# A diffusion trunk of two layers: the second layer's strips requested one to a step from the context's fifteenth step on, and four of its eight normalised beside later products

## Chip, cores and metric

The kernel runs on one core of a Trainium2 chip. Its time is in device microseconds (us), from one execution to the next of the same program; the number compared is the median of three runs. The profile is of one further execution, and all places in it are given in us from the start of its span.

## The reference

A trunk of two layers works on 1024 latent tokens of width 1024 (a grid of 16 rows of 64) with 256 context tokens before them. The first layer mixes tokens by attention and a linear recurrence, the second by neighbourhood attention on the grid. Around each mixer and each feed-forward part stand a root-mean-square norm and a modulation (scale and shift, computed from a conditioning vector). What the change touches is the end of the first layer's feed-forward part and the start of the second layer:

```python
# layer 0, end: feed-forward part of the latent and the context tokens
x   = x   + g2  * rms_norm(conv_ffn(h_lat, ...), norm_post_ffn[0])
ctx = ctx + g2c * rms_norm(conv_ffn(h_ctx, ...), norm_post_ffn[0])
# layer 1, start
h_lat = rms_norm(x,   norm_pre_mix[1]) * (1.0 + sc1)  + sh1
h_ctx = rms_norm(ctx, norm_pre_mix[1]) * (1.0 + sc1c) + sh1c
qkv   = h_lat @ w_qkv        # and h_ctx @ w_qkv; the values v are computed first
```

All matrix products are made from three products of halves (hi by hi, hi by lo, lo by hi): a tile read from memory, the raw tile, is split by ScalarE (ACT), which casts the high half, and by VectorE (DVE), which subtracts it for the low half.

## The kernel before

TensorE (PE), ACT, DVE, GpSimd (POOL) and the queue of SyncE (SP), which issues nearly all loads, each run their instructions in the order in which the program was written. In the part at hand that holds for SP too: a request that has to wait holds up every request behind it. Requests on SP take one of eight completion semaphores in turn, so that a request also waits until the one that last used its semaphore has landed.

**The down projection of the first layer** (`ffn_down`) ends with the context tokens, which are done as 22 steps, one for each block of 128 rows of the weight (`d_rawB`, 512 KB). I number them 0 to 21. A step has 12 matmuls: 2 blocks of tokens by 2 halves of the columns by 3. Its high and low halves are `d_Bh`, `d_Bl` (weight) and `d_Ah`, `d_Al` (activations, read from `actd` once for four steps, `d_rawA`, 512 KB). The products of the steps 18 to 21 are written as one pass of 48 matmuls at step 18; the 12 positions of the loop after that have no products. At each step the program also prepares the split four steps ahead and requests the weight two steps further ahead. `d_rawB` has three buffers, so the request for step k waits until the split of step k-3 has ended. The places for the halves of weights go round five.

Meanwhile the finished latent rows leave: DVE scales them and adds the old rows (`y`, `y_x`), and POOL issues their store into the scratch tensor `x2d`. When the context's products have ended, four pieces (`d_ps`, two blocks by two halves) are squared by ACT (line 1581), copied by DVE (line 1707), scaled and stored in turn. The accumulators come free with the last copy.

**The second layer's input** is `x2d`, read as eight strips `n_x` of 128 rows each, 512 KB (line 1733). Strip i holds every eighth row, beginning with row i, because the second layer works on 8 by 8 patches of the grid; so each strip needs all eight stores of latent rows. A strip is normalised in place by `odd_norm`: ACT squares and sums it (`junk`, line 1742), DVE adds epsilon (`rs_e`, line 120), POOL takes the power (`rs_r`, line 121), DVE multiplies (line 1745). `odd_norm` is a generator that gives way once for each strip and twice more.

`odd_early` is that work as a generator; the loop of the context's steps advances it once in each step (`next(other)`), after the step's other requests.

**`odd_values`** computes the second layer's values. `modulate(0, (0, 1, 2, 3), 0)` transposes the first four strips on PE (`n_pt<-ident,n_x`), ACT applies scale and shift (`n_t`), DVE splits (`xh`, `xl`). Eight weight pieces `w_raw` (512 KB, three buffers) are split into `w_hi`, `w_lo`. `products` multiplies tiles of 128 tokens: 24 matmuls a tile and half of the columns (`g_ps`), in eight yields of three matmuls. `mixed` takes one turn from each of its generators, and `both(a, b, n)` one turn of `b` after every n yields of `a`. The second four strips are modulated beside the products of the first four, the context tiles 8 and 9 beside those of the second four.

Of the kernel before, what the change touches and what calls it, by code (L numbers as in the profile page):

```python
# [13 lines left out]
BF16 = mybir.dt.bfloat16  # L14
# [6 lines left out]
P = 128  # L21
D = 1024
# [38 lines left out]
class Trunk:  # L61
# [1688 lines left out]
    def odd_early(self, nx, junk):  # L1750

        self.odd_x = {}
        for _ in range(9):
            yield
        for i in range(8):
            self.odd_load(nx, i)
        for _ in range(2):
            yield
        yield from self.odd_norm(range(8), junk)

    def odd_values(self, nx, xh, xl, gp, tp, sp):

        nc, a = self.nc, self.a
        sh, sc = self.mod[1, 0], self.mod[1, 1]
        wv = a["w_qkv"].rearrange("(k p) n -> p k n", p=P)
        raws, W = {}, {}

        def load(m):  # L1770
            if m < 8:
                raws[m] = self.wp.tile([P, 1024], F32, name="w_raw", bufs=3)
                k, c = 2 * (m % 4), 2048 + 512 * (m // 4)
                nc.sync.dma_start(raws[m].rearrange("p (a b) -> p a b", a=2), wv[:, k:k + 2, c:c + 512])

        def prepare(m):
            raw = raws.pop(m)
            hi, lo = (self.wp.tile([P, 1024], F32R, name="w_" + x, bufs=8) for x in ("hi", "lo"))
            nc.scalar.copy(hi, raw)
            nc.vector.tensor_tensor(out=lo, in0=raw, in1=hi.bitcast(F32), op=OP.subtract)  # L1780
            W[m] = hi, lo
            load(m + 3)

        def modulate(n0, tiles, s):
            n = P * len(tiles)
            for k in range(KT):
                pt = tp.tile([P, 512], F32, name="n_pt", tag="tp")
                for i, t in enumerate(tiles):
                    nc.tensor.transpose(pt[:, i * P:(i + 1) * P], self.odd_x[t][:, k * P:(k + 1) * P], self.ident)
                t = sp.tile([P, 512], F32, name="n_t", bufs=2)  # L1790
                nc.scalar.activation(t[:, :n], pt[:, :n], AF.Identity, scale=sc[:, k, s:s + 1], bias=sh[:, k, s:s + 1])
                nc.vector.tensor_copy(xh[:, k, n0:n0 + n], t[:, :n])  # L1792
                nc.vector.tensor_tensor(out=xl[:, k, n0:n0 + n], in0=t[:, :n], in1=xh[:, k, n0:n0 + n].bitcast(F32),
                                        op=OP.subtract)
                yield

        late = []

        def leave(ps, t, c):
            vs = sp.tile([P, 8, 2, HD], F32R, name="cv_st", bufs=2)  # L1800
            pv = ps.rearrange("p (h e) -> p h e", h=8)
            nc.scalar.copy(vs[:, :, 0, :], pv)
            yield
            nc.vector.tensor_tensor(out=vs[:, :, 1, :], in0=pv, in1=vs[:, :, 0, :].bitcast(F32), op=OP.subtract)
            yield
            nc.gpsimd.dma_start(self.vcd[t][:, 1024 * c:1024 * (c + 1)].bitcast(F32), vs.rearrange("p a b c -> p (a b c)").bitcast(F32))

        def products(tiles):

            for c in range(2):  # L1810
                for t in tiles:
                    ps = gp.tile([P, 512], F32, name="g_ps")
                    for k in range(KT):
                        wh, wl = (w[:, 512 * (k % 2):512 * (k % 2) + 512] for w in W[4 * c + k // 2])
                        xhk, xlk = xh[:, k, t * P:(t + 1) * P], xl[:, k, t * P:(t + 1) * P]
                        self.mm(ps, xhk, wh, k == 0, False)
                        self.mm(ps, xhk, wl, False, False)
                        self.mm(ps, xlk, wh, False, k == KT - 1)
                        if late and next(late[0], "end") == "end":
                            late.pop(0)  # L1820
                        yield
                    late.append(leave(ps, t, c))

        def both(a, b, n):

            for i, _ in enumerate(a):
                if i % n == n - 1:
                    next(b, None)
            for _ in b:
                pass  # L1830

        def mixed(*gens):
            gens = list(gens)
            while gens:
                for g in list(gens):
                    if next(g, "end") == "end":
                        gens.remove(g)
                    yield

        def context():  # L1840
            for i in (8, 9):
                self.odd_load(nx, i)
            junk = sp.tile([P, D], BF16, name="junk", bufs=1)
            yield
            yield
            yield from self.odd_norm((8, 9), junk)
            yield from modulate(SEQ, (8, 9), 1)

        def splits():
            for m in range(4, 8):  # L1850
                yield prepare(m)

        with self.in_order(*self.compute, mybir.EngineType.SP):
            for m in range(3):
                load(m)
            first = products((0, 1, 2, 3))
            for k, _ in enumerate(modulate(0, (0, 1, 2, 3), 0)):
                if k % 2 == 0:
                    prepare(k // 2)
                if k >= 2:  # L1860
                    next(first)
            both(first, mixed(splits(), modulate(512, (4, 5, 6, 7), 0)), 4)
            both(products((4, 5, 6, 7)), context(), 3)
            both(products((8, 9)), iter(()), 1)
            for g in late:
                for _ in g:
                    pass
# [445 lines left out]
```

## Time and profile before

| what | value |
|---|---|
| runs | 3455.88, 3460.55, 3461.36 us; median 3460.55 us |
| profiled execution | 3454.39 us |
| span of its trace | 3452.5 us, 48745 instructions |
| PE busy | 3137.3 us (91% of the span) |
| DVE, ACT, POOL busy | 2060.1, 1485.8, 1528.3 us |
| the part at hand | context's steps and the change of layer, about 1953 to 2140 us |

The profiled execution lies 6.2 us below the median of the runs, and its span 1.9 us below its own time. In the views, "idle before <-X" is the time in which an engine stood still before an instruction, with what ended it; `SPq` is SP's queue of requests; `PE` rows are matmuls and `PEld` rows the loads of the stationary operand beside them. The shares of the whole span say little on a part of 190 us; the part is read from the rows of that part.

### The profile page before, as it was taken

What the parts mean: (1) busy time and instruction counts of PE and PEld (TensorE: products, weight loads), DVE (VectorE), ACT (ScalarE), POOL (GpSimd) and SP (SyncE); (2) the same over time, 40 slices, a digit from 0 to 9 for tenths busy, and PEclk for the clock granted to TensorE, in tenths of its full rate; (3) what the DMA queues carried; (4) which work ended last, traced back from release to release, by engine and by line L of the source; (5) the groups of instructions that cost most, each with busy time, mean ns of one, the idle gap of its engine ahead of it and who ended that gap; (6) DMA issues with size and microseconds to landing.
All of it is one profiled execution on the core that took longest, in us unless ns stands there. A gap on an engine that the chain in (4) does not pass through costs nothing.

```text
span 3452.5 us, 48745 instructions
## 1 busy us (share of the span) xinstructions
PE 3137.3 (91%) x18364; PEld 2560.9 (74%) x18364; DVE 2060.1 (60%) x3413; ACT 1485.8 (43%) x2619; POOL 1528.3 (44%) x1147
## 2 busy tenths in 40 slices
PE   5999998869997799999999969999997689999997
PEld 3766776658886588888888748898986468888785
DVE  3625666657775745444577852477775565454778
ACT  3223222266663534343344442466674344333443
POOL 1310111187774476666510111577771167777201
PEclk7999999889999799999999989999999799999998
DMA  6533333321113112121285662222215412222756
GB/s 231 159 104 128 129 112 114 120 69 39 50 44 103 61 68 72 68 72 67 98 286 207 238 199 111 70 64 61 68 44 181 143 56 85 73 86 80 264 184 216
DMA packets 203948, 399.25 MB, mean 116 GB/s; under 512 B 23216, under 2 KB 85168, under 8 KB 203712
## 3 DMA queue, kind: packets, MB, share of 16 engines
q1 hardware_dynamic: 194656, 364.15, 32.0%
q0 software_dynamic: 9056, 31.99, 2.4%
q8 instruction: 144, 2.36, 0.3%
q14 instruction: 92, 0.75, 0.1%
HBM read 322.11 MB, written 74.34 MB: 115 GB/s over the span
## 4 chain that ended last, share of the span: by engine, by line
PE 73%; DVE 11%; DMA 5%; ACT 4%; issue 4%; POOL 2%; SPq 0%; POOLq 0%; ACTq 0%; DVEq 0%
PE g_ps L113 21%; PE u_g L113 13%; PE d_ps L113 10%; PE u_v L113 10%; PE u_pc L113 3%; PE a_pv L113 2%; PE c_pv L113 2%; PE c_s L113 2%; PE c_pt L2022 2%; PE a_pt L926 2%; PE mod_ps L113 1%; DVE a_pl L928 1%; PE a_s L113 1%; DMA d_rawA<-actd 1%; DMA y_x<-x2d 1%
## 5 line engine op out<-in xcount | busy, mean ns | idle before, releaser
L121 POOL TENSOR_TENSOR rs_r<-rs_e,mhalf 128x1 f32<-128x1 f32 (+3 forms) x106 | 84.8, 800 | 1019.8 <-DVE rs_e L120 1019.7
L113 PE MATMUL d_ps<-d_Bh,d_Ah 128*128 128x512 f32 x704 | 276.5, 393 | 28.1 <-ACT d_Ah L1456 21.9
L113 PE MATMUL g_ps<-xh,w_hi 128*128 128x512 f32 (+1 forms) x704 | 277.4, 394 | 6.4 <-ACT w_hi L543 6.4
L113 PE MATMUL d_ps<-d_Bl,d_Ah 128*128 128x512 f32 x704 | 277.4, 394 | 4.3 <-DVE d_Bl L1457 4.2
L113 PE MATMUL d_ps<-d_Bh,d_Al 128*128 128x512 f32 x704 | 276.4, 393 | 2.1 <-DVE d_Al L1457 1.9
L906 POOL TENSOR_SCALAR a_p<-a_p,rl 128x1280 f32<-128x1280 f32 (+1 forms) x80 | 240.1, 3004 | 70.5 <-DVE rl L905 62.3
L2005 POOL TENSOR_SCALAR c_p<-c_p,rl 128x640 f32<-128x640 f32 (+1 forms) x128 | 230.8, 1804 | 85.1 <-DVE rl L2004 60.5
L113 PE MATMUL g_ps<-xh,w_lo 128*128 128x512 f32 (+1 forms) x704 | 258.0, 367 | 1.2 <-DVE w_lo L544 1.2
L113 PE MATMUL g_ps<-xl,w_hi 128*128 128x512 f32 (+1 forms) x704 | 257.9, 366 | 0.0
L1238 DVE TENSOR_TENSOR f_u<-u_v,f_p 128x512 f32<-128x512 f32 x88 | 60.6, 688 | 199.0 <-PE u_v L113 199.0
L113 PEld LDWEIGHTS d_ps<-d_Bh,d_Ah 128*128 128x128 f32 x704 | 133.5, 190 | 57.8 <-ACT d_Ah L1456 23.2
L928 DVE TENSOR_TENSOR a_pl<-a_pt,a_ph 128x512 fp32r<-128x512 f32 (+1 forms) x200 | 118.6, 602 | 88.3 <-ACT a_ph L927 87.9
L113 PEld LDWEIGHTS g_ps<-xh,w_hi 128*128 128x128 f32 x704 | 134.3, 191 | 45.8 <-issue 27.5
L1224 POOL TENSOR_TENSOR w_S4l<-w_s,w_S4h 128x512 fp32r<-128x512 f32 x44 | 57.2, 1301 | 242.0 <-ACT w_S4h L1223 242.0
L113 PEld LDWEIGHTS d_ps<-d_Bl,d_Ah 128*128 128x128 f32 x704 | 133.3, 189 | 36.7 <-DVE d_Bl L1457 8.7
L113 PE MATMUL g_ps<-w_hi,xh 128*128 128x512 f32 (+1 forms) x400 | 156.6, 391 | 2.2 <-DVE xh L1792 1.2
L113 PEld LDWEIGHTS d_ps<-d_Bh,d_Al 128*128 128x128 f32 x704 | 133.2, 189 | 31.2 <-DVE d_Al L1457 3.3
L113 PE MATMUL g_ps<-w_lo,xh 128*128 128x512 f32 (+1 forms) x400 | 152.5, 381 | 3.7 <-DVE w_lo L1780 2.9
L927 ACT CAST a_ph<-a_pt 128x512 fp32r<-128x512 f32 (+1 forms) x200 | 102.7, 519 | 119.3 <-PE a_pt L926 119.2
L113 PEld LDWEIGHTS g_ps<-xh,w_lo 128*128 128x128 f32 x704 | 133.7, 190 | 25.3 <-DVE w_lo L544 1.7
L113 PE MATMUL g_ps<-w_hi,xl 128*128 128x512 f32 (+1 forms) x400 | 152.3, 381 | 0.2 <-DVE xl L278 0.2
L2025 DVE TENSOR_TENSOR c_pl<-c_pt,c_ph 128x256 fp32r<-128x256 f32 (+1 forms) x256 | 113.1, 470 | 50.5 <-ACT c_ph L2024 49.1
(468 smaller groups left out, 9729.3 us busy)
## 6 DMA issues: line engine op xcount, KB each, us to landing
m_raw<-in_w_mod SPq DMA_DIRECT2D x96, 512.0 KB
w_raw<-in_w_up SPq DMA_DIRECT2D x88, 512.0 KB
d_rawA<-actd SPq DMA_DIRECT2D x77, 512.0 KB
d_rawB<-in_w_down SPq DMA_DIRECT2D x74, 512.0 KB
actd<-f_t SPq DMA_DIRECT2D x22, 640.0 KB
d_t<-in_w_down SPq DMA_DIRECT2D x22, 512.0 KB
actd<-f_t SPq DMA_DIRECT2D x22, 512.0 KB
d_s<-actd SPq DMA_DIRECT2D x20, 512.0 KB
```

The source lines that it names most:

```text
L113: return self.nc.tensor.matmul(out, lhsT, rhs, start=start, stop=stop, skip_group_check=True, **k)
L121: nc.gpsimd.tensor_tensor(out=r[:p, :n], in0=e[:p, :n], in1=self.mhalf[:p, :n], op=OP.pow)
L906: nc.gpsimd.tensor_scalar(Pt[:, :nk], Pt[:, :nk], rl, None, op0=OP.mult)
L926: nc.tensor.transpose(pt[:, m, qt * P:(qt + 1) * P], Pt[:, kts[j + m] * P:(kts[j + m] + 1) * P], self.ident)
L927: nc.scalar.copy(ph[:, j:j + n], pt[:, :n])
L928: nc.vector.tensor_tensor(out=pl[:, j:j + n], in0=pt[:, :n], in1=ph[:, j:j + n].bitcast(F32), op=OP.subtract)
L1224: nc.gpsimd.tensor_tensor(out=lo, in0=part(j, name), in1=hi.bitcast(F32), op=OP.subtract)
L1238: nc.vector.tensor_tensor(out=out, in0=x, in1=y, op=OP.add)
L2005: nc.gpsimd.tensor_scalar(Pt[:, :n], Pt[:, :n], rl, None, op0=OP.mult)
L2022: nc.tensor.transpose(pt[:, j, :], Pt[:, (src + j) * P:(src + j + 1) * P], self.ident)
L2025: nc.vector.tensor_tensor(out=vap(pl, o, dims), in0=pt[:, :cnt], in1=vap(ph, o, dims).bitcast(F32), op=OP.subtract)
```

## The change

`odd_early` gave way nine times, requested all eight strips in the context's step 9, gave way twice more and then normalised all eight, one to a step. Now it gives way 14 times, and requests one strip in each of the steps 14 to 21. From the third strip on each of these turns also advances a normalisation, which covers strips 0 to 3 alone. Strips 4 to 7 are normalised in `odd_values`, by `second()`, ahead of their modulation and beside the products of the first four; there the turns come after every 3 yields, not every 4; the splits, norms and modulations take 19 turns (13 before), and 58 yields are left when they begin. The scratch tile `junk` of `odd_values` is allocated earlier for it.

```diff
     def odd_early(self, nx, junk):
         self.odd_x = {}
-        for _ in range(9):
-            yield
+        for _ in range(14):
+            yield
+        norm = self.odd_norm(range(4), junk)
         for i in range(8):
             self.odd_load(nx, i)
-        for _ in range(2):
-            yield
-        yield from self.odd_norm(range(8), junk)
+            if i >= 2:
+                next(norm)
+            yield
...
+        def second():
+            yield from self.odd_norm(range(4, 8), junk)
+            yield from modulate(512, (4, 5, 6, 7), 0)
...
-            both(first, mixed(splits(), modulate(512, (4, 5, 6, 7), 0)), 4)
+            both(first, mixed(splits(), second()), 3)
```

The first place is SP's order of requests in the context's steps: `d_rawB` and `d_rawA` are the down projection's tiles, `n_x` the strips, `y_x` the old rows of the two context tiles.

```order
-L1422 DMA d_rawB<-in_w_down 128x1024 x3
-L1733 DMA n_x<-x2d 128x1x1024 x8
-L1422 DMA d_rawB<-in_w_down 128x1024
+L1422 DMA d_rawB<-in_w_down 128x1024 x4
 L1422 DMA d_rawA<-actd 128x4x256
 L1422 DMA d_rawB<-in_w_down 128x1024 x4
 L1422 DMA d_rawA<-actd 128x2x256
+L1733 DMA n_x<-x2d 128x1x1024
 L1422 DMA d_rawB<-in_w_down 128x1024
+L1733 DMA n_x<-x2d 128x1x1024 x3
 L1594 DMA y_x<-x1d 128x1024 x2
+L1733 DMA n_x<-x2d 128x1x1024 x4
```

The eight strips stood together ahead of the weights of steps 16 to 21; now one stands ahead of the weight of step 21 alone, three behind it, and four behind the context's old rows and ahead of `w_raw`.

The second place is ACT at the end of the context's steps, with the casts of steps 13 to 21 and the squares of strips (`junk`).

```order
+L1456 CAST d_Bh<-d_rawB 128x1024 x4
+L1456 CAST d_Ah<-d_rawA 128x1024
+L1456 CAST d_Bh<-d_rawB 128x1024 x4
 L1456 CAST d_Ah<-d_rawA 128x512
 L1742 ACTIVATE junk,ms<-n_x 128x1024
 L1456 CAST d_Bh<-d_rawB 128x1024
+L1742 ACTIVATE junk,ms<-n_x 128x1024 x3
```

The square of strip 0 stands ahead of the last weight's cast, and the squares of strips 1 to 3 behind it, ahead of the squares of the context's pieces; before, one square stood ahead of the cast of step 16 and one behind each weight's cast from there on.

The third place is ACT beside the products of the first four tiles in `odd_values`, in the changed kernel: `w_hi` are casts of the weight pieces 4 to 7, `cv_st` the way out of a product.

```order
+L1780 CAST w_hi<-w_raw 128x1024
+L1742 ACTIVATE junk,ms<-n_x 128x1024
+L1780 CAST w_hi<-w_raw 128x1024
+L1803 CAST cv_st<-g_ps 128x8x64
+L1742 ACTIVATE junk,ms<-n_x 128x1024
+L1780 CAST w_hi<-w_raw 128x1024
+L1742 ACTIVATE junk,ms<-n_x 128x1024
+L1803 CAST cv_st<-g_ps 128x8x64
+L1780 CAST w_hi<-w_raw 128x1024
+L1742 ACTIVATE junk,ms<-n_x 128x1024
```

Four squares of strips (4 to 7) now stand here between the weight casts, and the modulation of these strips, which stood here before, follows them.

More of the change, by code (lines that the diff above doesn't have):

```diff
@@ L1842, in context @@
                 self.odd_load(nx, i)
-            junk = sp.tile([P, D], BF16, name="junk", bufs=1)
             yield
@@ L1851, in splits @@
                 yield prepare(m)
+        def second():
+            yield from self.odd_norm(range(4, 8), junk)
+            yield from modulate(512, (4, 5, 6, 7), 0)
+        junk = sp.tile([P, D], BF16, name="junk", bufs=1)
         with self.in_order(*self.compute, mybir.EngineType.SP):
```

## Prediction

> **What bounds the kernel now.** I read first the table of stages around the change of layer: from and to, length, then busy time (x instructions) of PE, PEld, DVE, ACT and POOL, granted PE clock, busy share of the DMA engines, GB/s.
>
> ```profile
> 1953.00:1990.90 37.90, 35.19 (x147) 26.86 (x145) 30.75 (x45) 17.25 (x28) 4.48 (x8) 1.00 0.67 230
> 1990.90:2012.80 21.90, 0.02 (x1) 0.00 (x0) 1.23 (x1) 3.27 (x5) 0.00 (x0) 0.55 1.04 264
> 2012.80:2034.20 21.40, 19.63 (x72) 14.49 (x72) 15.54 (x27) 14.13 (x24) 8.47 (x9) 0.90 0.40 139
> 2034.20:2038.90 4.70, 0.01 (x1) 0.01 (x1) 3.88 (x7) 1.38 (x4) 0.95 (x2) 0.87 0.31 102
> 2038.90:2055.50 16.60, 12.48 (x53) 9.53 (x54) 15.17 (x25) 9.77 (x12) 2.03 (x4) 0.73 0.67 221
> 2055.50:2130.00 74.50, 74.50 (x345) 59.94 (x345) 29.64 (x52) 23.67 (x36) 7.54 (x14) 1.00 0.31 113
> 1989.00:2007.00 18.00, 1.92 (x9) 1.26 (x7) 0.00 (x0) 1.15 (x2) 0.00 (x0) 0.62 1.03 233
> 2010.00:2013.00 3.00, 0.18 (x1) 0.18 (x2) 1.42 (x2) 2.32 (x3) 0.00 (x0) 0.50 0.98 374
> ```
>
> PE is the bound on both sides: 35.19 of 37.90 us in the context's steps, all 74.50 us in the values' products. Between them it stands for 21.90 us while the DMA engines are full, and 4.70 us at the change of layer. The two last rows show what fills the DMA: 233 GB/s while strips pass, 374 GB/s once weights pass. A strip of 524288 bytes so takes 2.25 us, a contiguous load of that size 1.40 us. Next I read the timeline around the long stop, and SP's waits.
>
> ```profile
> 1977.15 1.22 DVE L1457 TENSOR_TENSOR d_Bl<-d_rawB,d_Bh 128x1024 fp32r<-128x1024 f32 x1
> 1978.39 0.33 SPq L1422 DMA_DIRECT2D d_rawB<-in_w_down  x1
> 1979.42 1.22 DVE L1457 TENSOR_TENSOR d_Bl<-d_rawB,d_Bh 128x1024 fp32r<-128x1024 f32 x1
> 1982.49 1.06 ACT L1456 CAST d_Bh<-d_rawB 128x1024 fp32r<-128x1024 f32 x1 [3.02 <-DMA d_rawB<-in_w_down]
> 1984.10 2.35 DVE L1457 TENSOR_TENSOR d_Bl<-d_rawB,d_Bh 128x1024 fp32r<-128x1024 f32 x2
> 1987.50 5.53 SPq L1733 DMA_DIRECT2D n_x<-x2d  x8
> 1992.39 1.06 ACT L1742 ACTIVATE junk<-n_x 128x1024 bf16<-128x1024 f32 x1 [8.85 <-DMA n_x<-x2d]
> 1993.14 0.53 SPq L1422 DMA_DIRECT2D d_rawB<-in_w_down  x1
> 2010.33 1.04 ACT L1456 CAST d_Bh<-d_rawB 128x1024 fp32r<-128x1024 f32 x1 [16.79 <-DMA d_rawB<-in_w_down]
> 2012.82 0.79 PE L113 MATMUL d_ps<-d_Bh,d_Ah 128*128 128x512 f32 x1 [21.90 <-ACT d_Ah L1456]
> 2013.41 0.63 PE L113 MATMUL d_ps<-d_Bl,d_Ah 128*128 128x512 f32 x1
> ...
> SPq L1733 <- DMA x2d<-y: 8.5, 1, 8.5
> ```
>
> The split of step 12 ends at 1978.37 and frees its buffer; at 1978.39 SP requests step 15, which is there at 1982.49, 4.1 us later. Step 13's buffer is free at 1979.42 + 1.22 = 1980.64, but SP stands before the first strip (8.5 us, for the last store of latent rows), issues eight strips from 1987.50 and comes to step 16 only at 1993.14. Its weight then lies behind the strips: cast at 2010.33. So the 21.90 us are the price of the strips' place, not of PE, DVE or the amount of data.
>
> **The change, part by part.**
>
> *1. The strips leave SP's queue ahead of steps 16 to 20 (the gain).* By the rows above, step 16 is requested at 1980.64 and lands 4.1 us later, at 1984.7, its `d_rawA` 1.4 behind at 1986.1. DVE is free at 1984.10 + 2.35 = 1986.45; with 1.22 a low half, step 16's two are ready at 1988.9, ahead of PE, which ends step 15, its last before the stop, at 1990.9: that wait goes wholly. Step 17 is requested at 1985.3 (first of the pair), there at 1989.4, split at 1991.7 (+ 1.04 + 1.22); step 18 requested at 1986.45, there 1.4 behind 17 at 1990.8, split at 1993.1. A step costs PE 12 matmuls; the rate comes from two rows of the last pass, 24 matmuls apart: 5.44 / 24 = 0.227 us.
>
> ```profile
> 2020.63 0.62 ACT L1456 CAST d_Ah<-d_rawA 128x512 fp32r<-128x512 f32 x1
> 2022.70 0.68 DVE L1457 TENSOR_TENSOR d_Al<-d_rawA,d_Ah 128x512 fp32r<-128x512 f32 x1
> 2028.37 0.39 PE L113 MATMUL d_ps<-d_Bh,d_Al 128*128 128x512 f32 x1
> 2033.81 0.39 PE L113 MATMUL d_ps<-d_Bh,d_Al 128*128 128x512 f32 x1
> ```
>
> So PE starts step 17 at 1993.6 and the last pass (steps 18 to 21) at 1996.35, each time after its split.
>
> *2. One strip stands ahead of step 21, in SP's and in ACT's queue.* Step 20 is requested when 17 is split, 1991.7, and lands at 1995.8, its half-size `d_rawA` 0.7 later at 1996.5; its last low half is ready at 1998.8 (casts 1.04 and 0.62, low halves 1.22 and 0.68). Strip 0 lands 2.25 later, at 1998.75; step 21, requested at 1993.1, behind it at 2000.15. ACT squares strip 0 meanwhile (1.06 and 0.19 for the sum, done at 2000.0), so that square is hidden by step 21's transfer; without that cover it costs 1.25. Cast 2001.2, low half 2002.4. PE would reach step 21's second matmul (the 11th of 48) at 1998.6: it waits about 3.8 us in all. Its 38 last matmuls then end at 2002.4 + 37 x 0.227 + 0.39 = 2011.2, against 2033.81 + 0.39 = 2034.2: 23.0 us earlier. Within these, the slow matmuls after the long stop (0.63 us, not 0.39) are gone too.
>
> *3. Strips 1 to 3 and the way out of the context.* They lie behind step 21: strip 3 lands at 2000.15 + 3 x 2.25 = 2006.9. All four scalings stand ahead of the first copy on DVE, the squares ahead of the context's on ACT.
>
> ```profile
> 2024.58 1.06 ACT L1742 ACTIVATE junk<-n_x 128x1024 bf16<-128x1024 f32 x1
> 2025.55 0.19 ACT L1742 ACTIVATION_READ_ACCUMULATOR junk<-n_x 128x1 f32 x1
> 2029.44 0.15 DVE L120 TENSOR_SCALAR rs_e<-ms 128x1 f32<-128x1 f32 x1
> 2030.31 0.75 DVE L1745 TENSOR_SCALAR n_x<-n_x,rs_r 128x1024 f32<-128x1024 f32 x1 [0.73 <-POOL rs_r L121]
> 2030.98 0.68 DVE L1707 COPY y<-d_ps 128x512 f32<-128x512 f32 x1
> 2032.42 0.69 DVE L1707 COPY y<-d_ps 128x512 f32<-128x512 f32 x1 [0.76 <-ACT yjunk L1581]
> 2035.01 0.69 DVE L1707 COPY y<-d_ps 128x512 f32<-128x512 f32 x1 [1.65 <-ACT yjunk L1581]
> 2038.89 2.82 PE L1789 MATMUL n_pt<-ident,n_x 128*128 128x128 f32 x12 [4.69 <-DVE yms L315]
> ```
>
> Square 1.25, then 2030.31 + 0.75 - 2029.44 = 1.62 from epsilon to scaled strip: the first copy can start at 2009.8. Copy to copy takes 1.44 when PE is done, and from the third copy to the transposes 3.88: 2009.8 + 1.44 + 1.44 + 3.88 = 2016.6. By the products alone it would be 2011.2 + 4.7 = 2015.9; the later one counts. The transposes start 22.3 us earlier than at 2038.89, and the strips take back 0.7.
>
> *4. Strips 4 to 7 ahead of the first weight piece.* On the DMA follow two `y_x` (1.4 each), four strips, `w_raw` 0: 2006.9 + 2.8 + 9.0 + 1.4 = 2020.1.
>
> ```profile
> 2040.72 1.03 ACT L1779 CAST w_hi<-w_raw 128x1024 fp32r<-128x1024 f32 x1
> 2041.16 1.29 DVE L1584 TENSOR_TENSOR y<-y,y_x 128x512 f32<-128x512 f32 x2
> 2042.93 0.77 PE L113 MATMUL g_ps<-w_hi,xh 128*128 128x512 f32 x1 [1.22 <-DVE xh L1792]
> 2043.42 1.22 DVE L1780 TENSOR_TENSOR w_lo<-w_raw,w_hi 128x1024 fp32r<-128x1024 f32 x1
> ```
>
> Before, its cast stood 1.83 us after the first transpose, which would be 2018.4 now: 1.7 late. But DVE is held by the context's second block and reaches the low half only 4.53 after the transpose, at 2021.1, and the late cast ends at 2021.15. I cost it at 0.1; if DVE came sooner it would cost up to 1.7. `w_raw` 1 waits for that second block as before.
>
> *5. Norms of strips 4 to 7 beside the products.* ACT gets 4 x 1.25, DVE 4 x 0.90, POOL four powers, in a stage of 74.50 us where ACT is busy 23.67 and DVE 29.64; PE waits for none of them unless a strip is late, and these land at 2018.7 while their first transpose comes after 36 yields of 3 x 74.50 / 345 = 0.65 us, near 2057. The last modulation turn comes at yield 57 of 58; its result is needed seven yields (4.5 us) later and takes one ACT and two DVE instructions, on that row's means 0.66 + 2 x 0.57 = 1.8. Cost 0; it fails only if turns slip by over 2 us. The `junk` tile moves no request and adds no wait that ends late.
>
> *Sum.* 23.0 - 0.7 - 0.1 = 22.2 us. The profiled execution of 3454.39 would become 3432.2 (its span 3452.5, 3430.3). It lay 6.2 below the median of 3460.55, so I forecast 3438.3.
>
> **The unknown price** is a strip's time S when strips are asked for singly. Below: 1.40, the contiguous load. Above: 4.89, a lone strip from its request (1987.50) to its first use (1992.39). I take 2.25, since eight in flight ran at that rate and here too the next is requested before the last has landed. The time of the first `w_lo` is then 1996.5 + 8 S + 5.6 + 1.04, and the gain 2043.42 less that: 40.3 - 8 S, or 22.3 at 2.25 and 1.2 at 4.89; at 1.40 the products bind and it is 23.8.
>
> The stop of 3.8 us at step 21 may also slow PE's clock: after 21.90 us the next matmuls took 0.63 and after 4.69 (the first product of the layer) 0.77. Ten slow ones cost some 2 us of the products, 2013.2 + 4.7 = 2017.9 for the transposes, so 1.3 less gain (3439.6). The Trainium skill, "TensorE: Matmul & The Clock Gate", section "What's actually happening", says that the clock halves after about one idle window of 3.4 us, free-running; by that rule this would happen about every second time, and the trace so far agrees on the two longer stops and shows none between.
>
> **Rivals.**
>
> *Each strip pays part of its own start.* For it: the lone strip's 4.89. Against: 18 us at a steady 233 GB/s. Midway, S = 3.57: gain 11.7, so 3448.8. The Trainium skill, "DMA: Bandwidth & Descriptors", section "Anatomy of one DMA — SWDGE (gpsimd) path", puts about 2.0 us of fixed time on a DMA that GpSimd issues (SP issues these); if each strip paid it alone, S would be an estimated 3.2 and the time 3445.9. This trace's strips, at 2.25 in a row, do not bear it out.
>
> *No change.* SP's 8.5 us wait before the first strip shows that stores matter too; if step 16 were held by something else, the stop would stay. Against it stands the request at 1993.14, straight behind the strips. S near 4.9 gives the same: 3459.4.
>
> *Slower.* The first weight piece of the second layer is behind all eight strips, and PE has nothing else to do there. From S = 40.3 / 8 = 5.04 the move costs more than the stop did; at S = 6.0 the time is 3468.2. For it: this order has four strips and two loads directly in front of an idle PE, where before only 4.70 us stood open. Against it: a strip would have to take over twice as long as in any run of strips above.
>
> **How the numbers follow.** Forecast with a full clock 0.60, with a slowed one 0.18 (0.78 together); own start 0.11; no change 0.05; slower 0.06. Faster by over 0.2% (6.9 us, about what a measurement of this kernel can tell from no change) takes the first two: 0.89. Range: from 3436.8 (S = 1.40) less the runs' spread below their median (4.7), 3432, up to the own-start rival, 3449.
>
> **What would show it.** Right: SP's first strip near 1992.5 and not before step 20; no PE stop of over 5 us among the steps; PE waiting 3 to 4 us for step 21; transposes at 2016 to 2018; no wait beside the products after them. Wrong: ACT waiting for `n_x` long after the products' end, or `w_hi` waiting several us for `w_raw` 0.

## The result, and the profile after

The changed kernel took 3439.3 us (median of 4 executions, 3432.7 to 3442.52), the kernel before beside it 3458.22 us (4 executions, 3453.98 to 3461.36): a ratio of 0.9944, 95% interval 0.9924 to 0.9964. Run again later, in five executions, it took 3442.72 us, a ratio of 0.9958 [0.9946, 0.9971]. All nine have a median of 3442.44 us; 43 executions of the kernel before, over all comparisons, one of 3457.76 us. So the change is worth about 15 us. The forecast of 3438.3 us lies within 1 us of the first median, but that closeness is partly luck: the gain that it summed, 22.2 us, is some 7 us larger than the one measured, and the median that it started from, 3460.55 us, is 2.8 us above that of all executions of before. Against the nine executions it is 4.1 us too low. What follows asks where the rest of the gain went.

The profiled execution of the changed kernel took 3442.52 us, with a span of 3440.7 us. First the table of stages, cut as before: from and to, length, busy time (x instructions) of PE, PEld, DVE, ACT and POOL, granted clock, DMA share, GB/s.

```profile
1957.31:1995.20 37.89, 35.66 (x151) 27.78 (x150) 33.03 (x47) 19.92 (x31) 4.48 (x8) 1.00 0.83 288
1995.20:2021.61 26.41, 20.40 (x72) 14.95 (x71) 11.68 (x18) 11.19 (x18) 2.76 (x5) 0.81 0.94 231
2021.61:2026.30 4.69, 0.00 (x1) 0.00 (x0) 3.87 (x7) 1.38 (x4) 0.94 (x2) 0.94 0.98 230
2026.30:2043.00 16.70, 12.31 (x53) 9.62 (x54) 15.15 (x26) 9.91 (x12) 2.05 (x4) 0.81 0.69 232
2043.00:2117.40 74.40, 74.40 (x344) 59.92 (x344) 32.24 (x60) 27.64 (x44) 9.87 (x18) 1.00 0.31 114
```

The row of 21.90 us in which PE stood is gone, and the change of layer (4.69) and the values' products (74.40) are as long as before although DVE and ACT now do four norms beside the products. But the steps after the stop, 21.40 us before, take 26.41 us, at a granted clock of 0.81. The timeline shows where.

```profile
1981.46 1.22 DVE L1457 TENSOR_TENSOR d_Bl<-d_rawB,d_Bh 128x1024 fp32r<-128x1024 f32 x1
1998.07 0.58 SPq L1733 DMA_DIRECT2D n_x<-x2d  x1
1998.75 0.53 SPq L1422 DMA_DIRECT2D d_rawB<-in_w_down  x1
2000.73 1.05 ACT L1456 CAST d_Bh<-d_rawB 128x1024 fp32r<-128x1024 f32 x1 [2.48 <-DMA d_rawB<-in_w_down]
2005.67 1.06 ACT L1742 ACTIVATE junk<-n_x 128x1024 bf16<-128x1024 f32 x1 [3.36 <-DMA n_x<-x2d]
2007.94 1.05 ACT L1456 CAST d_Bh<-d_rawB 128x1024 fp32r<-128x1024 f32 x1 [1.12 <-DMA d_rawB<-in_w_down]
2009.04 0.80 PE L113 MATMUL d_ps<-d_Bh,d_Ah 128*128 128x512 f32 x1 [4.84 <-ACT d_Bh L1456]
2010.30 0.80 PE L113 MATMUL d_ps<-d_Bl,d_Ah 128*128 128x512 f32 x1 [0.46 <-DVE rs_e L120]
2010.89 0.63 PE L113 MATMUL d_ps<-d_Bh,d_Al 128*128 128x512 f32 x1
2014.60 1.06 ACT L1742 ACTIVATE junk<-n_x 128x1024 bf16<-128x1024 f32 x1 [0.95 <-DMA n_x<-x2d]
2016.01 0.39 PE L113 MATMUL d_ps<-d_Bh,d_Ah 128*128 128x512 f32 x1
2026.30 2.82 PE L1790 MATMUL n_pt<-ident,n_x 128*128 128x128 f32 x12 [4.69 <-DVE y L1707]
2029.07 1.05 ACT L1780 CAST w_hi<-w_raw 128x1024 fp32r<-128x1024 f32 x1 [0.83 <-DMA w_raw<-in_w_qkv]
2030.84 1.22 DVE L1781 TENSOR_TENSOR w_lo<-w_raw,w_hi 128x1024 fp32r<-128x1024 f32 x1
```

The first row is step 12's low half, at which this part begins in both kernels (1977.15 before). Up to there the two programs are the same, yet it starts anywhere from 1973.1 to 1983.9 us in the fourteen traces of this study (1975.2 to 1983.9 us in the four that one and the same chip gave); so I count from it and write t for the time since. Strip 0's square waits 3.36 us for its strip, step 21's cast behind it 1.12 us for its weight, and PE stands 4.84 + 0.46 us. Then it runs slow matmuls (0.80, 0.63 us) for 5 us before it is back at 0.39. The products end at t+40.15, the transposes start at t+44.84. Before, that was t+57.1 and t+61.74, so 16.9 us were gained here. The first `w_lo` follows the transposes by 4.54 us (4.53 before).

### The profile page after: what moved, and what is told of

The parts are those of the page before. It is cut to its first block, busy times and chain, and to the rows that moved or that the text cites. A ratio compares the mean times of both kernels' runs of the same rounds, so it can differ in the third digit from the quotient of the medians.

```text
span 3440.7 us, 48748 instructions
## 1 busy us (share of the span) xinstructions
PE 3141.5 (91%) x18364; PEld 2565.3 (75%) x18364; DVE 2058.2 (60%) x3413; ACT 1486.8 (43%) x2619; POOL 1525.8 (44%) x1147
## 4 chain that ended last, share of the span: by engine, by line
PE 75%; DVE 10%; DMA 4%; ACT 4%; issue 4%; POOL 2%; SPq 0%; POOLq 0%; ACTq 0%; DVEq 0%
PE g_ps L113 21%; PE u_g L113 13%; PE d_ps L113 11%; PE u_v L113 10%; PE u_pc L113 3%; PE a_pv L113 2%; PE c_pv L113 2%; PE c_s L113 2%; PE c_pt L2028 2%; PE a_pt L926 2%; PE mod_ps L113 1%; DVE a_pl L928 1%; PE a_s L113 1%; ACT a_ph L927 1%; DMA y_x<-x2d 1%
```

## The experiments

One correction first. The description of the kernel ahead says that a strip holds every eighth row. By the view at line 1733 it holds 16 runs of 8 adjacent rows (32 KB each), 256 KB apart. That all eight stores of latent rows must have landed before any strip holds either way; what an expectation below says on the step between rows is to be read so.

| kernel | median us (executions) | ratio to before [95%] | step 21's cast | PE stops there | products' end | transposes |
|---|---|---|---|---|---|---|
| before | 3457.76 (43) | | | 21.90 | t+57.1 | t+61.74 |
| changed | 3439.3 (4) | 0.9944 [0.9924, 0.9964] | t+26.48 | 5.30 | t+40.15 | t+44.84 |
| changed, again | 3442.72 (5) | 0.9958 [0.9946, 0.9971] | t+25.83 | 4.79 | t+39.5 | t+44.2 |
| strip 0 behind step 21 | 3439.88 (4) | 0.9946 [0.9929, 0.9963] | t+23.56 | 2.58 | t+37.0 | t+43.2 |
| eight normed early | 3447.44 (1) | | t+26.43 | 4.96 | t+40.1 | t+54.2 |
| four normed, requests as before | 3459.9 (1) | | | 21.13 | t+56.2 | t+60.9 |
| strips of adjacent rows | 3437.0 (1) | | t+23.24 | 2.14 | t+36.1 | t+40.8 |
| strip 0 one turn earlier | 3433.22 (5) | 0.9922 [0.9910, 0.9934] | t+23.52 | 2.79 | t+37.5 | t+42.2 |
| four behind step 21 | 3437.98 (5) | 0.9937 [0.9925, 0.9950] | t+25.22 | 4.48 | t+37.8 | t+42.5 |
| strip 0 two turns earlier | 3435.65 (5) | 0.9934 [0.9920, 0.9948] | t+21.80 | 1.15 | t+34.7 | t+39.4 |
| ... and its square behind step 21 | 3436.64 (5) | 0.9943 [0.9930, 0.9955] | t+22.15 | 1.44 | t+33.4 | t+38.1 |
| one turn earlier, square behind | 3437.37 (5) | 0.9942 [0.9929, 0.9956] | t+23.88 | 1.59 | t+37.2 | t+41.8 |
| row pitch of 1088 | 3440.8 (5) | 0.9958 [0.9944, 0.9971] | t+24.58 | 4.45 | t+37.2 | t+41.8 |
| runs close together | 3440.47 (4) | 0.9954 [0.9933, 0.9974] | t+25.65 | 4.57 | t+39.3 | t+44.0 |

The ratios are to the executions of before in the same comparison. "There" is step 21; in the two kernels with the requests in step 9 it is step 16. The times t are from one profiled execution each; the products' end is the transposes' start less PE's idle time there. The executions of one changed kernel spread over 2.9 to 11.5 us, so the readings rest on t. But t has a spread of its own: the two traces of the changed kernel and that with the runs close together, which has the same instructions in the same order, put the transposes at t+44.0 to t+44.8, and that with the row pitch, which has this order too, at t+41.8. A difference of 2 to 3 us between two single traces is therefore not sure.

**Is it the requests or the norms?** The diff has two halves. This kernel has only the second: requests and first four norms from step 9 as before, the last four norms beside the products.

```diff
-        for _ in range(14):
+        for _ in range(9):
             yield
-        norm = self.odd_norm(range(4), junk)
         for i in range(8):
             self.odd_load(nx, i)
-            if i >= 2:
-                next(norm)
-            yield
+        for _ in range(2):
+            yield
+        yield from self.odd_norm(range(4), junk)
```

> The requests as before (all eight in step 9), and only the other part of the change: strips 0 to 3 normalised early, 4 to 7 beside the products. Theory (the stop comes from the requests alone): PE stands 21 to 22 us for step 16, transposes at +61 to +62.5 from step 12's low half as before, time within 0.1% of the kernel before. Rival (ACT and DVE at the end of the context's steps cost something too): transposes at +60 or earlier.

```profile
2018.71 0.79 PE L113 MATMUL d_ps<-d_Bh,d_Ah 128*128 128x512 f32 x1 [21.13 <-ACT d_Ah L1456]
2044.72 1.54 PE L1789 MATMUL n_pt<-ident,n_x 128*128 128x128 f32 x6 [4.69 <-DVE y L1707]
```

The stop is back (21.13 us), and the transposes start at t+60.9, within 1 us of before: the split of the norms alone brings nothing that can be told from the spread. The other half alone, requests as changed but all eight norms in the context's loop:

```diff
-        norm = self.odd_norm(range(4), junk)
+        norm = self.odd_norm(range(8), junk)
...
+        yield from norm
...
-            yield from self.odd_norm(range(4, 8), junk)
...
-            both(first, mixed(splits(), second()), 3)
+            both(first, mixed(splits(), second()), 4)
```

> The changed kernel's requests, but all eight strips normalised in the context's loop, ahead of the context's way out, and the modulation of the second four as before. Counted from step 12's low half. Theory (every square that stands ahead of the copies makes them wait for its strip): strip 7 lands near +44, the first copy starts near +47, transposes at +52 to +54 against +44.8, so 7 to 9 us of the gain are lost. Rival (only the requests' place matters, the norms are hidden anyway): transposes at +45, time as the changed kernel's.

```profile
2008.29 1.06 ACT L1742 ACTIVATE junk<-n_x 128x1024 bf16<-128x1024 f32 x1 [0.57 <-DMA n_x<-x2d]
2014.82 1.06 ACT L1742 ACTIVATE junk<-n_x 128x1024 bf16<-128x1024 f32 x1 [5.38 <-DMA n_x<-x2d]
2030.20 1.12 PE L1791 MATMUL n_pt<-ident,n_x 128*128 128x128 f32 x4 [14.12 <-DVE y L1707]
```

ACT waits 5.38 us between strip 3 (first row) and strip 4, with the squares of the context's pieces queued behind, and PE stands 14.12 us instead of 4.69. The requests make the gain, and the split of the norms keeps 9.3 us of it (t+54.2 against t+44.84; 7 to 9 were expected).

**What does strip 0 ahead of step 21 cost?** All eight strips one turn later:

```diff
-        for _ in range(14):
+        for _ in range(15):
```

> The changed kernel with the strips one step later (steps 15 to 22), so that strip 0 stands behind the weight of step 21; strip 3 then comes to stand behind the two y_x. Times are counted from the start of step 12's low half on DVE, ahead of anything that is moved (before: products end +57.1, transposes start +61.7; changed: +40.2 and +44.8). Theory (the stop at step 21 is the strip's place, but the strips' chain stands close behind it): no stop of over 1 us at step 21, products end near +32, strip 3 lands some 2.8 us later than in the changed kernel, and the transposes start at +44 to +46, so no gain over the change. Rival (the stop and the slow clock after it are all that the change lost): transposes at +37, 7.8 us earlier than in the changed kernel.

```profile
1998.78 1.04 ACT L1456 CAST d_Bh<-d_rawB 128x1024 fp32r<-128x1024 f32 x1 [2.90 <-DMA d_rawB<-in_w_down]
1999.88 0.79 PE L113 MATMUL d_ps<-d_Bh,d_Ah 128*128 128x512 f32 x1 [2.11 <-ACT d_Bh L1456]
2009.28 1.06 ACT L1742 ACTIVATE junk<-n_x 128x1024 bf16<-128x1024 f32 x1 [3.88 <-DMA n_x<-x2d]
2018.40 0.90 PE L1790 MATMUL n_pt<-ident,n_x 128*128 128x128 f32 x3 [6.21 <-DVE y L1707]
```

Step 21's cast comes 2.9 us earlier and PE's stop shrinks to 2.11 + 0.47 us, but strip 3 now lies behind the two `y_x` loads, ACT waits 3.88 us for it, and PE gives back half of it at the change of layer (6.21, not 4.69): of 3.2 us at the products' end 1.7 are left. The products' end, expected near t+32, came at t+37.0, and the stop that was to stay under 1 us is 2.58: even with no strip in front, step 21's weight is late. Why it is late no run shows; the strips requested right behind it may hold it.

With strip 3 in front of the `y_x` loads again, both ends should come:

```diff
-        for _ in range(14):
+        for _ in range(15):
             yield
...
-        for i in range(8):
+        self.odd_load(nx, 0)
+        for i in range(1, 8):
```

> Strips 0 and 1 are both requested right behind step 21's weight, 2 and 3 in the next two turns, so that strip 3 is again ahead of the two y_x loads. Theory (strip 0 in front of step 21 costs a stop, strip 3 behind the y_x costs 5 us on its chain; this order pays neither): squares of strips 0 to 3 at about t+25, 27, 29 and 31, first copy t+34, products' end t+37 as where strip 0 alone stood behind step 21, transposes 4.7 behind them at t+41.7, 3 us less than the change, about 3436. Rival (the strips' chain binds whenever all four are behind step 21): transposes t+43 or later.

```profile
2004.39 1.06 ACT L1742 ACTIVATE junk<-n_x 128x1024 bf16<-128x1024 f32 x1 [3.77 <-DMA n_x<-x2d]
2005.45 1.03 ACT L1456 CAST d_Bh<-d_rawB 128x1024 fp32r<-128x1024 f32 x1
2006.53 0.79 PE L113 MATMUL d_ps<-d_Bh,d_Ah 128*128 128x512 f32 x1 [4.01 <-ACT d_Bh L1456]
2022.72 0.69 PE L1791 MATMUL n_pt<-ident,n_x 128*128 128x128 f32 x2 [4.69 <-DVE y L1707]
```

The squares fell where expected and the transposes at t+42.5, near the t+41.7 expected and within 3 us of the change, so that the gain itself is not sure. But here strip 0 was behind step 21 in SP's queue and still ahead of it in ACT's: ACT waited 3.77 us for the strip with step 21's cast behind, which then started without any wait, at t+25.2. Where request and square had both gone behind step 21 (all eight strips one turn later), that cast came at t+23.6. So a request and its first use have to be moved together.

**Strip 0 further ahead.** One turn earlier, and two:

```diff
-        for _ in range(14):
+        for _ in range(13):      # two turns: range(12)
             yield
...
             self.odd_load(nx, i)
+            if i == 0:
+                yield            # two turns: twice
```

> Strip 0 is requested one turn earlier, ahead of step 20's weight; no strip is requested in the next turn; strips 1 to 7 as in the change. Times from the start of step 12's low half (t). Theory (step 21 was late because a strip of 4.0 us with its start stood in front of it; one turn earlier most of that start passes beside weights whose buffers are full): step 20's cast about t+21 (19.3 in the change), step 21's t+23 to 24 (26.5), stops of 2 to 3 us in all (5.3), products' end t+36 to 37.5 (40.2), transposes t+41 to 42 (44.8), so 3 to 4 us less than the change, about 3436. Rival (there is no slack one turn earlier either, the strip's whole time comes out of PE wherever it stands): transposes t+44.5 to 45.5, no difference to the change.

> Strip 0 is requested two turns earlier than in the change, ahead of step 19's weight, none in the two turns after it. Theory as for one turn earlier: steps 19 and 20 take the strip's time with the slack that they have, step 21's cast t+23 to 24, stops of 1 to 3 us in all, products' end t+35.5 to 37.5, transposes t+40 to 42. Rival (steps 19 and 20 have no slack, and the stop only moves forward in the pass): stops of 4 to 5 us ahead of step 19 or 20, transposes t+44 or later.

Of one turn:

```profile
2001.43 1.04 ACT L1456 CAST d_Bh<-d_rawB 128x1024 fp32r<-128x1024 f32 x1 [1.94 <-DMA d_rawB<-in_w_down]
2002.53 0.67 PE L113 MATMUL d_ps<-d_Bh,d_Ah 128*128 128x512 f32 x1 [2.20 <-ACT d_Bh L1456]
2020.08 1.33 PE L1792 MATMUL n_pt<-ident,n_x 128*128 128x128 f32 x5 [4.69 <-DVE yms L315]
```

Of two turns:

```profile
1996.03 0.51 PE L113 MATMUL d_ps<-d_Bh,d_Ah 128*128 128x512 f32 x1 [0.39 <-ACT d_Bh L1456]
1997.29 0.51 PE L113 MATMUL d_ps<-d_Bl,d_Ah 128*128 128x512 f32 x1 [0.76 <-DVE rs_e L120]
1998.74 0.63 PE L113 MATMUL d_ps<-d_Bh,d_Ah 128*128 128x512 f32 x1
2012.50 0.90 PE L1793 MATMUL n_pt<-ident,n_x 128*128 128x128 f32 x3 [4.69 <-DVE y L1707]
```

The times speak against both rivals: stops of 2.8 and 1.15 us, transposes at t+42.2 and t+39.4. One turn missed its range by 0.2 us; two turns came 0.6 us earlier than theirs. Not all of the theory held: step 20's cast, expected near t+21 with the strip in front of it, came at t+19.0, no later than in the change. With two turns step 19's cast came 2.0 us later than in the change (t+17.7) and PE did not stand for it. So steps 19 and 20 had slack for a strip, and step 21 had none. That step 21's cast came earlier with two turns (t+21.8) than with no strip in front of it at all (t+23.6) this does not explain; it stays open. Of two turns the profile puts the last wait down to `rs_e`, strip 0's epsilon. I took it to stand in front of step 21's low half on DVE, which is a misreading: that low half starts at 1996.01 us and `rs_e` at 1997.15, behind it. On ACT the square did stand directly in front of step 21's cast. So I also moved the norms one turn later:

```diff
-            if i >= 2:
+            if i >= 3:
+                next(norm)
+            if i == 7:
                 next(norm)
```

> Strip 0 is requested two turns earlier than in the change (ahead of step 19's weight), and the norms start one turn later, so that strip 0's square (ACT) and its epsilon (DVE) stand behind step 21's cast and low half. Times from the start of step 12's low half (t). Theory (with strip 0 two turns earlier the last 1.15 us of stop come from strip 0's norm in front of step 21 on ACT and DVE, and any stop of this size costs some 2 us more by a slow clock): step 21's cast at t+20 to 21 (21.8), stops under 0.6 us in all, matmuls of the last pass at 0.39 us, products' end t+32 to 33.5 (34.7), strips' chain now binding: first copy t+31 to 32, transposes t+37.5 to 38.5 (39.4). Rival (step 21's weight is what is late): stop of 1 us or more as before, transposes t+39 to 40.

```profile
2001.02 1.05 ACT L1456 CAST d_Bh<-d_rawB 128x1024 fp32r<-128x1024 f32 x1 [1.48 <-DMA d_rawB<-in_w_down]
2002.12 0.49 PE L113 MATMUL d_ps<-d_Bh,d_Ah 128*128 128x512 f32 x1 [0.68 <-ACT d_Bh L1456]
2003.37 0.50 PE L113 MATMUL d_ps<-d_Bl,d_Ah 128*128 128x512 f32 x1 [0.76 <-DVE rs_e L120]
2003.71 0.39 PE L113 MATMUL d_ps<-d_Bh,d_Al 128*128 128x512 f32 x1
2016.97 2.82 PE L1795 MATMUL n_pt<-ident,n_x 128*128 128x128 f32 x12 [4.69 <-DVE yms L315]
2021.01 0.77 PE L113 MATMUL g_ps<-w_hi,xh 128*128 128x512 f32 x1 [1.22 <-DVE xh L1798]
```

The mechanism was wrong and the time right. The cast waits 1.48 us for its weight, so with the square out of its way the weight is what is late; the stops did not shrink (0.68 + 0.76; "rs_e" is still named, and again the low half is what ended then), and the strips' chain does not bind (4.69 us at the transposes). But the matmuls after the stops ran at 0.39 us at once, and that brought the transposes to t+38.1. Why they did, the granted clock shows in the last section.

The same edit on the version of one turn, and the changed kernel once more beside them:

> As the version with strip 0 one turn earlier (ahead of step 20's weight), with the norms one turn later. Theory (there the weight of step 21 was late, its cast idle 1.94 us for it; the square was not in the way): step 21's cast t+23 to 23.5, stops of 2 to 2.8 us, transposes t+41.5 to 42.5, no difference to 42.2. Rival (strip 0's norm was in the way here too): transposes t+40.5 or earlier.

> The changed kernel once more, for a direct comparison with the two versions beside it: about 3439, as it was; transposes t+44 to 46, stops of 4.5 to 5.5 us in all. If the earlier strip 0 is worth what the traces say, the version with it two turns earlier is 4 to 7 us below this.

The first came to t+41.8, no real difference from t+42.2, as the theory said (PE stood 1.44 us for step 20 and 1.13 + 0.46 us for step 21). The changed kernel fell at t+44.2. In that comparison all five executions of the version with strip 0 two turns earlier and its square behind (3434.38 to 3441.67) lie below all five of the changed kernel (3441.9 to 3444.76): 6.1 us between the medians (4 to 7 expected), and 6.1 between their t. It beats both kernels. The version of one turn beats the changed kernel by ratio (0.9934 at most, against 0.9946 at least for the changed kernel run again), though its t+42.2 alone would not show it. Among the versions with strip 0 earlier the ratios do not follow t: the lowest, 0.9922, belongs to t+42.2 and 0.9943 to t+38.1. So which of them is best is not shown.

**Why is a strip slow?** The first trial read 128 adjacent rows for a strip; it so normalises other tokens than the reference.

```diff
-            src = self.x2d[0:SEQ].rearrange("(r g i) d -> g r i d", g=8, i=8)[i]
+            src = self.x2d[i * P:(i + 1) * P]
```

> The changed kernel, but each strip reads 128 rows that lie together, where it should read every eighth row; tokens stand in another order in the second layer. Theory (the strips are slow since their rows lie 32 KB apart): strips follow each other by 1.3 to 1.5 us and not by 2.2 to 2.3, the stop at step 21 falls from 4.84 to 3 to 4 us, strip 3 lands 3 to 4 us earlier. Rival (they are slow since they read what was just stored, or for their place in the queue): 2.2 us a strip as before, nothing moves by over 0.5 us.

```profile
2006.13 1.06 ACT L1742 ACTIVATE junk<-n_x 128x1024 bf16<-128x1024 f32 x1
2007.41 1.06 ACT L1742 ACTIVATE junk<-n_x 128x1024 bf16<-128x1024 f32 x1
2004.68 0.51 PE L113 MATMUL d_ps<-d_Bh,d_Ah 128*128 128x512 f32 x1 [1.38 <-ACT d_Bh L1456]
2021.13 1.12 PE L1790 MATMUL n_pt<-ident,n_x 128*128 128x128 f32 x4 [4.69 <-DVE y L1707]
```

Strips so read are squared 1.28 us apart with no wait for the DMA, against 2.1 to 2.3 us. A square with its sum takes ACT 1.06 + 0.19 us, so this is ACT's own pace, and the load takes no longer. The stop at step 21 falls to 1.38 + 0.76, more than expected, and the transposes to t+40.8. Is it the place of the rows, or the form of the request? First, the same rows with another pitch, so that the runs do not stand a power of two apart:

```diff
-        self.x2d = d("x2d", [NTOK, D])
+        self.x2d = d("x2d", [NTOK, D + 64])[:, 0:D]
```

> The changed kernel with one number changed: rows of the scratch tensor x2d lie 1088 floats apart, not 1024, so that its rows stay 4 KB long but the 16 runs of 8 rows that a strip reads stand 272 KB apart, not 256 KB. Every engine's instructions are the same and in the same order. Times from the start of step 12's low half (t). Theory (the strip of adjacent rows was fast because its parts did not stand at a large power of two from each other; nothing else about the strip is slow): squares of strips 1 to 3 follow each other by 1.3 to 1.6 us (2.2), strip 0's square t+21.3 to 22.3 (24.2), transposes t+40 to 41.5 (44.8), 3 to 4.5 us less than the change, so 3436 to 3439 beside 3442 for the change. Rival (sixteen separate runs are slow wherever they stand, or rows just stored are): squares 2.1 to 2.3 apart, transposes t+44 to 45.5.

```profile
2005.26 1.06 ACT L1742 ACTIVATE junk<-n_x 128x1024 bf16<-128x1024 f32 x1 [0.85 <-DMA n_x<-x2d]
2007.43 1.06 ACT L1742 ACTIVATE junk<-n_x 128x1024 bf16<-128x1024 f32 x1 [1.02 <-DMA n_x<-x2d]
```

Still 2.17 us apart: my theory of the power of two fell. (The transposes came at t+41.8, since strip 0 was there sooner, at t+22.6; in the three other traces of this order it was t+23.2 to t+24.2. Whether the pitch has a part in that, one trace does not show; the five executions, at a ratio of 0.9958, show no gain.) Last, the same form with the runs close together:

```diff
-            src = self.x2d[0:SEQ].rearrange("(r g i) d -> g r i d", g=8, i=8)[i]
+            src = self.x2d[120 * i:120 * i + 144].rearrange("(r q) d -> r q d", q=9)[:, 0:8]
```

> The changed kernel; a strip again reads 16 runs of 8 rows in a request of the same form, but the runs start 9 rows (36 KB) apart instead of 64 (256 KB), so nearly all adjacent; it normalises other tokens than the reference for that. Times from the start of step 12's low half (t). Theory A (what costs is the request's form, 16 runs of 8 rows that can't be joined to one run of 128): squares of strips 1 to 3 follow each other by 2.1 to 2.3 us, strip 0's square t+22.5 to 24.5, transposes t+41.5 to 45. Theory B (what costs is how far apart the runs lie in memory): squares 1.3 to 1.5 apart, strip 0's square t+21.3 to 22, transposes t+40 to 41.5, as with the joined run.

```profile
2007.62 1.06 ACT L1742 ACTIVATE junk<-n_x 128x1024 bf16<-128x1024 f32 x1 [0.68 <-DMA n_x<-x2d]
2009.74 1.06 ACT L1742 ACTIVATE junk<-n_x 128x1024 bf16<-128x1024 f32 x1 [0.97 <-DMA n_x<-x2d]
```

2.12 us apart with the runs 36 KB from each other: it is the form, 16 runs of 8 rows that do not join to one run of 128, and not where they lie. What in the form does it stays open.

## Why the prediction was right, and where its sum was off

- *The stop and its cause*: right. The 21.90 us were the strips' place in SP's queue; with the requests put back alone they return (21.13 us).
- *The strip's time S*: 2.25 us was right for strips in a row (2.23 us from step 21's cast to strip 1's square, then 2.33 and 2.10 us from square to square), so "own start for each strip" (3.57) and the slower case (above 5.04) fell. It was mis-sized for strip 0: step 20's cast was 0.6 us later than summed, and strip 0's square came at t+24.2, not t+21.6, so behind step 20's activations it took about 2.0 us more than S. Over the four traces of this order it came from t+22.6 to t+24.2; with strips of adjacent rows it came at t+21.5, so this excess, too, goes with the strip's form. How is open.
- *Step 21 behind it*: mis-sized by 0.9 us; it followed strip 0 by 2.27 us, not 1.40. With the two terms above its cast came at t+26.5 instead of t+23.0, and PE's stop was 4.84 + 0.46 us instead of 3.8.
- *The slowed clock*, which the prediction set aside with 0.18 against 0.60, came true, and in all four traces of this order. Its working was off as well: a stop of 3.8 us holds a wholly idle window of 3.41 us (the beat of the granted clock in these traces) only about once in nine times (0.39 of 3.41), not every second time; the traces show that a window need not be idle (last section). From the second wait's end the last 38 matmuls took 2021.61 - 2010.30 = 11.31 us instead of 8.8: 2.5 us. 3.5 us for the cast and 2.5 for the clock are the 6.0 by which the products ended late (t+40.15 for t+34.1).
- *The strips' chain binds, 0.7 us behind the products*: wrong. With the products 6.0 us later and the chain 3.2 later (first copy t+35.9 for t+32.7), the products bind, so that the transposes missed by 5.4 us (t+44.84 for t+39.45). The profile's sign of it is the idle time of 4.69 us at the transposes; where the chain did bind, with strip 0 behind step 21, it was 6.21. Two of the signs named for being right failed with these terms: PE waited 5.3 us at step 21, not 3 to 4, and the transposes lay outside 2016 to 2018 us, which is t+38.9 to t+40.9.
- *`w_raw` 0 late and hidden*: right. Its cast waited 0.83 us for the DMA, and `w_lo` stood 4.54 us behind the transposes as before.
- *Norms beside the products at no cost*: right, 74.40 us against 74.50.
- *From the part to the whole*: 16.9 us gained here, 11.8 us in the span (3452.5 less 3440.7). The part began 4.3 us later in this trace than in that of before and what follows the transposes' start took 0.8 us longer, though the products in it are no longer (74.40 us). The prediction took one trace's distance to the median (6.2 us) as given; over 43 executions it is 3.4.

## What to carry to other kernels

When a queue holds transfers for later among those for now, work out for each place in the queue which consumer has slack: here the same strip in front of step 19 and not of step 21 was worth 5 us (t+39.4 against t+44.2 and t+44.8). Move a request and its first use together, since an in-order engine that waits for the early one holds back everything that is already there. And where a sum leaves a short stop of PE open, add the slow matmuls behind it, and compare t from a common point, not whole spans, when code far away moves by more than the effect.

## What the runs showed of the hardware

A stop of PE cost more than its length, and its length did not decide how much. After 4.84 + 0.46 us (changed kernel) and after only 0.39 + 0.76 us (strip 0 two turns earlier) ten and eight matmuls ran at about 0.63 instead of 0.39 us, 2.5 and 1.7 us lost; after 0.68 + 0.76 us (two turns earlier with the square behind) none did. Likewise the first product of the layer took 0.77 us in that last trace and 0.47 in the repeated changed kernel, after the same stops of 4.69 and 1.22 us:

```profile
2028.39 0.47 PE L113 MATMUL g_ps<-w_hi,xh 128*128 128x512 f32 x1 [1.22 <-DVE xh L1793]
```

The granted clock tells why. In all fourteen traces it is either 1.00 or 0.50, and every stretch of either is a whole multiple of 3.41 us long: it changes on a beat. It fell to 0.50 in 337 places, and in the beat ahead of each PE was busy for at most 2.17 of 3.41 us. (A beat as empty as that does not always bring it down: the emptiest that did not had 1.49 us of matmuls.) Two beats each of strip 0 two turns earlier, and of the same with the square behind, in the columns of the table of stages:

```profile
1994.92:1998.33 3.41, 2.16 (x7) 1.24 (x7) 1.73 (x4) 2.20 (x3) 0.56 (x1) 1.00 1.03 245
1998.33:2001.75 3.42, 3.42 (x10) 2.67 (x9) 1.96 (x5) 1.41 (x3) 1.10 (x2) 0.50 1.01 295
1998.40:2001.81 3.41, 2.64 (x8) 0.99 (x6) 2.38 (x3) 1.93 (x3) 0.00 (x0) 1.00 0.99 290
2001.81:2005.23 3.42, 2.35 (x9) 1.75 (x10) 2.10 (x4) 2.52 (x6) 0.70 (x2) 1.00 1.06 270
```

In the first trace one beat took in both stops, PE was busy for 2.16 of 3.41 us, and the next beat ran at 0.50. In the second trace the beat changed at 2001.81 us, within the first stop; PE was busy for 2.64 and 2.35 us, more than ahead of any fall, and the clock stayed at 1.00. In the changed kernel it fell to 0.50 at 2005.23 us, after a beat with 1.67 us of matmuls and before the stop of 4.84 us had ended. The first products differ in the same way: the clock was 0.50 from 2015.47 to 2025.71 us where the product took 0.77 us, and 1.00 from 2027.15 to 2030.56 us where it took 0.47. So a short stop costs more than itself when it falls into one beat, and where it falls is luck. Of the twelve traces with stops of 1.15 to 5.30 us at step 21, eleven show slow matmuls behind them.

The Trainium skill, "TensorE: Matmul & The Clock Gate", section "What's actually happening", has a clock that halves after an idle window of about 3.4 us, in windows that run free of the kernel. The beat of these traces agrees with the windows; but a window with 2.16 us of matmuls was far from idle, so by these traces it need not be idle to halve the clock.

A load of 128 rows of 4 KB took 2.1 to 2.3 us as 16 runs of 8 rows and at most 1.28 us as one run of 128, with the DMA engines full in both: 233 GB/s at a share of 1.03 while strips passed in the kernel before, and 414 GB/s at 1.02 with strips of adjacent rows, in this row:

```profile
2003.00:2007.00 4.00, 1.87 (x5) 1.11 (x5) 1.59 (x3) 3.07 (x4) 0.56 (x1) 0.91 1.02 414
```

The traces hold packets of 4096 bytes for both forms; in these two stretches a packet took 0.30 us at the median as 16 runs and 0.16 us as one run. The Trainium skill, "DMA: Bandwidth & Descriptors", section "Why a DMA increments its semaphore by 16 and not by 1", spreads a load over as many engines, up to 16, as divide its outermost sizes; by that rule 16 runs and 128 rows are both spread over 16, and the shares of 1.03 and 1.02 of 16 engines agree. So the number of engines does not explain the difference, and the cause stays open.

Identical code ahead of the change took up to 10.8 us more or less from one trace to the next (t's start at 1973.1 to 1983.9 us, over several chips; up to 8.6 us on one of them).
